# A two-layer trunk on one core: other rooms for the last output weights, and the last norms queued after the last tile

## The chip, the cores and the metric

The kernel runs on one core of one Trainium2 chip. The metric is device time in microseconds (us). A core has TensorE (PE, matmuls and transposes into PSUM, with the weight loads shown apart as PEld), VectorE (DVE), ScalarE (ACT) and GpSimd (POOL), and here SyncE (SP) issues nearly all the loads, with 16 DMA engines that move the bytes. Each engine takes its instructions in the order of its own queue and waits on semaphores for others.

## The reference

The trunk has two layers over 1024 positions of 1024 channels. Layer 0 mixes with an S5 scan and a GLU, layer 1 with a short gated convolution. Each is followed by the same FFN and a gated per-layer input (called ple below):

```python
for i in range(DEPTH):                      # DEPTH = 2
    hn = rmsnorm(h, norm_mix_g[i])
    mix = s5_mixer(hn, ...) if i % 2 == 0 else shortconv_mixer(hn, ...)
    h = h + mix
    h = h + swiglu_ffn(rmsnorm(h, norm_ffn_g[i]), ffn_w_in[i], ffn_w_out[i])
    gate = sigmoid(rmsnorm(h, norm_ple_g[i]) @ ple_w_gate[i])
    h = h + gate * (p[i] @ ple_w_up[i])
return rmsnorm(h, final_norm_g)
```

The hidden width of the FFN is 2816, and all of it is float32.

## The kernel before

**Precision and tiles.** Every matrix product is made from float32 operands split in two: `hi` is a cast (ACT, L87) and `lo` the remainder (a DVE subtraction, L88), and `mm3` (L122 to L124) adds three matmuls hi·hi, hi·lo and lo·hi. The 1024 positions are 8 tiles `t` of 128, taken in the order 0, 4, 1, 5, 2, 6, 3, 7. Tiles q and q+4 form pair q.

**Stages, by the trace.** S5 scan to about 225 us, GLU to 407, first FFN half (`ffn_in`) 420 to 848, second half (`ffn_out`) 848 to 1112, ple 1112 to 1206, then in layer 1 `conv_in` 1225 to 1470, `conv_out` 1480 to 1557, `ffn_in` 1571 to 1997, `ffn_out` 1998 to 2262, ple and the final norm to the end.

**The seven-product stages.** `ffn_in` and `conv_in` compute 2x2 blocks with seven products instead of eight (`block_product`). Their moving operands c = 0 to 6 are made from the normed tiles by `norm_pair` (L207): for each pair two scalings `xn` on DVE (L173), 16 transposes on PE (L181), four DVE subtractions (L221 to L232), and seven splits called `put(0)` to `put(6)`, each a cast on ACT and a subtraction on DVE (L88). c = 0 to 3 lie in `ulow`, c = 4 to 6 in `uhigh`. A product of one block is 12 matmuls. The weights come as two loads `raw` and are made into seven operands `ws` by casts, sums and splits (L275 to L283, L87, L88).

**The output stages.** `out_phase` (L326) serves `ffn_out` and `conv_out`. It keeps weight rows as split "units" in SBUF and runs through them in groups; for `ffn_out` these are units 0 to 7, 8 to 15 and 16 to 21, in `conv_out` 0 to 3 and 4 to 7. For each group it goes over the eight tiles: load the hidden activations (`ch`, one or two chunks of four units, L346), in group 0 also load the residual `h` (L348), multiply, and add into `h` on DVE (L360). In the last group the tile's sum of squares (L139) and `last_post` (L366) follow. The units of the next group are fetched (L330) while the group runs, one after each tile, if their room is free ("early"), otherwise after the group's last tile. The rooms are eight slots in `ulow` (units 0 to 7), six in `uhigh` (8 to 13), four in `s8` (14 to 17), and for units 18 to 21 again four of `uhigh`, which group 1 is still reading, so these four are late. The four gate units of ple take `uhigh` slots 4, 5, 0, 1, two early and two late.

**One ring for all loads.** Weights (`raw`), chunks (`ch`) and normed tiles (`xn`) share four slots r0 to r3 of a ring (`raw_tile`, L82), taken in turn in the order in which the program allocates them. A load's issue on SP waits for the last reader of its slot, and every DMA issue behind it on SP waits too.

**What orders the work.** The program's order and a list scheduler that works through a timeline give each engine its fixed queue; `first()` raises the priority of the sums and norms. `posted()` (L1010) makes `last_post`: where seven products follow, pair q's work is placed after tile q+1, and pair 3's after tile 7. Where ple follows, each tile's norm (`norm_tile`, into `s8` tiles) is placed after that tile.

Of the kernel before, what the change touches and what calls it, by code (L numbers as in the profile page):

```python
# [23 lines left out]
def trunk(  # L24
# [11 lines left out]
    T = S // P  # L36
# [95 lines left out]
    def square(t, cs):  # L132

        if "ms" not in squares:
            squares["ms"] = tiny.tile([P, T, 4], F32, name="ms", tag="ms")
        got = squares.setdefault(t, [])
        junk = t2_tile("junk", BF16, D)
        ms = squares["ms"][:, t, len(got):len(got) + 1]
        A.activation(junk[:, cs], h[t][:, cs], AF.Square, scale=1.0 / math.sqrt(D), accum_out=ms)  # L139
        got.append(ms)  # L140
# [66 lines left out]
    def norm_pair(q, gb):  # L207
        t0, t1 = q, q + HT
        halves = 2 if q == HT - 1 else 1
        x0, x1 = normed(t0, gb, halves), normed(t1, gb, halves)  # L210

        def put(c, src):
            split(moving_part(c, 0, q), moving_part(c, 1, q), by_kt(src))

        p11, p12, p22 = transposed(x0, 0), transposed(x1, 0), transposed(x1, 1)
        p21 = transposed(x0, 1, mm)
        put(0, p11)
        b12 = t2_tile("b12")
        A.copy(b12, p12)
        T1 = t2_tile("T1")  # L220
        V.tensor_tensor(T1, b12, p11, ALU.subtract)  # L221
        T2 = t2_tile("T2")
        V.tensor_tensor(T2, p22, T1, ALU.subtract)
        put(1, T2)
        put(2, T1)
        put(3, p21)
        T3 = t2_tile("T3")
        V.tensor_tensor(T3, p22, b12, ALU.subtract)
        put(4, T3)
        put(5, p22)  # L230
        T4 = t2_tile("T4")
        V.tensor_tensor(T4, p21, T2, ALU.subtract)  # L232
        put(6, T4)

# [54 lines left out]
    def block_product(ws, on_c11=None):  # L289


        def prod(ps, i, start):
            for kt in range(KH):
                sl = slice(kt * P, (kt + 1) * P)
                mm3(ps, ws[i][:, 0, sl], ws[i][:, 1, sl], moving(i, kt, 0), moving(i, kt, 1),
                    start and kt == 0, kt == KH - 1, more=not start)

        a = psum()
        prod(a, 0, True)
        s1 = ev_tile("s1")  # L300
# [25 lines left out]
    def out_phase(wout, groups, last_post, following=()):  # L326
# [4 lines left out]

        units = {ht: fetch(ht, room) for ht, room, _ in groups[0]}
        for gi, group in enumerate(groups):
# [5 lines left out]
            for t in ORDER:  # L339
# [7 lines left out]
                if gi == 0:  # L347
                    nc.sync.dma_start(out=h[t], in_=hdram[t])  # L348
                ps = [psum() for _ in range(2)]
                for j in parts:  # L350
                    mine = [x[0] for x in group if x[0] // 4 == j]
                    for nb in range(2):
# [5 lines left out]
                        if mine[-1] == group[-1][0]:  # L358
                            with first():
                                V.tensor_tensor(h[t][:, cs], ps[nb], h[t][:, cs], ALU.add)  # L360
                                if last:
                                    square(t, cs)
                if soon:
                    soon.pop(0)()
                if last:
                    last_post(t)  # L366
            for f in soon + late:
                f()

    def room_low(q, s):  # L370
# [25 lines left out]
    def ffn_out(l, post, following):  # L396
        rooms = [(room_low(q, s), False) for s in range(2) for q in range(HT)]
        rooms += [(room_high(i), True) for i in range(6)] + [(room_new(i), True) for i in range(4)]
        rooms += [(room_high(i), False) for i in range(4)]
        hts = [(ht, *room) for ht, room in enumerate(rooms)]  # L400
# [15 lines left out]
    def ple(l, units, post):  # L416
        more, makers = ple_units(l, 1, [room_new(i) for i in range(4)])
        for nb in range(2):
# [3 lines left out]
            for t in ORDER:  # L422
# [3 lines left out]
                for c0, c1 in ((0, 256), (256, 512)) if last else ((0, 512),):  # L426
# [4 lines left out]
                    with first():  # L431
                        A.activation(ps, ps, AF.Sigmoid)
                        V.tensor_tensor(upt[:, c0:c1], ps, upt[:, c0:c1], ALU.mult)
                        hc = slice(nb * 512 + c0, nb * 512 + c1)
                        V.tensor_tensor(h[t][:, hc], upt[:, c0:c1], h[t][:, hc], ALU.add)
                        square(t, hc)
# [44 lines left out]
    def glu(post):  # L481
# [3 lines left out]
        for nb in range(4):  # L485
# [8 lines left out]
            for t in ORDER:  # L494
# [5 lines left out]
                with first():  # L500
                    A.activation(sg, ps[:, 256:512], AF.Sigmoid)
                    V.tensor_tensor(sg, ps[:, 0:256], sg, ALU.mult)
                    V.tensor_tensor(h[t][:, cs], sg, h[t][:, cs], ALU.add)
                    square(t, cs)
# [505 lines left out]
    def posted(gain, pairs):  # L1010

        gb = load_gain(gain)

        def pair(q):
# [4 lines left out]
        def post(t):  # L1019
            if not pairs:  # L1020
                return norm_tile(t, gb)
            if 0 < t < HT:
                pair(t - 1)
            if t == T - 1:
                pair(HT - 1)
        return post
# [73 lines left out]
```

## Time and profile before

| | |
|---|---|
| Median of 3 runs | 2356.33 us (2354.39 to 2356.82) |
| Profiled execution | 2359.43 us, its span 2357.5 us |
| Mean granted TensorE clock | 0.981 |
| PE busy | 2247.0 us, 95% of the span |
| PEld, DVE, ACT, POOL busy | 78%, 56%, 32%, 7% |
| DMA moved | 288.87 MB, mean 123 GB/s |

PE's queue is busy for nearly the whole span, so time that is to be had lies in the stretches where PE stands still or where the clock granted to it is the lower of its two levels, 1.2 instead of 2.4 GHz (0.5 in the rows). A row of the timeline gives the start, the duration, the engine and line, the operation, and in brackets the idle time before it and what ended that. Matmuls overlap, so the pitch from start to start, and not the duration, is what one costs.

### The profile page before, as it was taken

The page shows a single profiled execution, that of the slowest core. Times are in us where ns is not written, and L with a number is a line of the kernel's source. Part 1 is how long each engine was busy: PE and PEld are TensorE (multiplying, and loading weights), DVE is VectorE, ACT ScalarE, POOL GpSimd, SP SyncE. Part 2 cuts the span into 40 slices and gives each one's busy share as a digit, 9 for nine tenths or more (in the row PEclk, how much of TensorE's full clock was granted, in tenths as well). Part 3 has the DMA queues.
Part 4 walks back from the last instruction along what each step waited for, and adds up shares of the span by engine and source line. Part 5 has one row for each costly group of instructions (what it writes and reads, how often), then busy time and mean ns, then how long its engine had stood idle before and what let it go on. Part 6 is the DMA issues. An engine that isn't in the chain of part 4 may idle for free.

```text
span 2357.5 us, 27090 instructions
## 1 busy us (share of the span) xinstructions
PE 2247.0 (95%) x10253; PEld 1835.7 (78%) x10253; DVE 1331.9 (56%) x2246; ACT 765.5 (32%) x1449; POOL 163.1 (7%) x268
## 2 busy tenths in 40 slices
PE   6888999899999999999979999989999999999998
PEld 4776887788888878878858888768888888788787
DVE  7785326866666642125488776487666666121454
ACT  6554223433333320013343332153333333000232
POOL 2110001000000000000000000010000001000000
PEclk8999999999999999999989999999999999999999
DMA  7555202333333364333232225434333335543333
GB/s 246 141 135 148 69 1 89 105 112 112 111 114 110 107 241 149 118 127 114 70 129 81 90 92 179 159 125 125 108 108 107 111 113 172 212 139 107 108 109 110
DMA packets 212978, 288.87 MB, mean 123 GB/s; under 512 B 21360, under 2 KB 152432, under 8 KB 212848
## 3 DMA queue, kind: packets, MB, share of 16 engines
q1 hardware_dynamic: 191520, 212.63, 29.0%
q0 software_dynamic: 20928, 74.47, 10.2%
q8 instruction: 80, 1.31, 0.2%
q14 instruction: 50, 0.41, 0.1%
q10 hardware_dynamic: 400, 0.04, 0.0%
HBM read 190.93 MB, written 79.69 MB: 115 GB/s over the span
## 4 chain that ended last, share of the span: by engine, by line
PE 85%; DMA 6%; DVE 5%; ACT 1%; SPq 1%; issue 1%; POOL 0%; DVEq 0%; POOLq 0%; ACTq 0%
PE psmm L122 27%; PE psmm L124 27%; PE psmm L123 27%; DMA ch<-hid 2%; PE pstr L181 1%; DMA raw<-in_ffn_w_out_dram 1%; DMA tw<-tmp 1%; DVE W L575 1%; DVE gv L925 1%; DMA h<-hd 1%; DVE tmp L575 1%; DVE ulow L88 1%; DVE uhigh L88 1%; PE pstr L874 0%; DVE raw L575 0%
## 5 line engine op out<-in xcount | busy, mean ns | idle before, releaser
L122 PE MATMUL psmm<-ulow,ws 128*128 128x512 f32 x896 | 351.1, 393 | 1.6 <-ACT s L301 1.6
L123 PE MATMUL psmm<-ulow,ws 128*128 128x512 f32 x896 | 350.6, 391 | 0.0
L124 PE MATMUL psmm<-ulow,ws 128*128 128x512 f32 x896 | 350.4, 391 | 0.0
L124 PE MATMUL psmm<-uhigh,ws 128*128 128x512 f32 x672 | 265.3, 395 | 0.0
L122 PE MATMUL psmm<-uhigh,ws 128*128 128x512 f32 x672 | 265.1, 394 | 0.0
L123 PE MATMUL psmm<-uhigh,ws 128*128 128x512 f32 x672 | 264.9, 394 | 0.0
L360 DVE TENSOR_TENSOR h<-psmm,h 128x512 f32<-128x512 f32 x128 | 88.0, 690 | 276.6 <-PE psmm L124 276.6
L88 DVE TENSOR_TENSOR ws<-raw,ws 128x512 fp32r<-128x512 f32 x224 | 153.6, 688 | 117.8 <-ACT ws L87 117.4
L87 ACT CAST ws<-raw 128x512 fp32r<-128x512 f32 x224 | 137.5, 619 | 213.0 <-PE psmm L124 211.2
L122 PEld LDWEIGHTS psmm<-ulow,ws 128*128 128x128 f32 x896 | 169.4, 189 | 39.5 <-ACT s L301 2.9
L123 PEld LDWEIGHTS psmm<-ulow,ws 128*128 128x128 f32 x896 | 169.4, 189 | 36.2
L124 PEld LDWEIGHTS psmm<-ulow,ws 128*128 128x128 f32 x896 | 169.2, 189 | 36.2
L87 ACT CAST ws<-st 128x512 fp32r<-128x512 f32 x168 | 104.0, 620 | 204.4 <-PE psmm L124 189.5
L123 PEld LDWEIGHTS psmm<-uhigh,ws 128*128 128x128 f32 x672 | 126.1, 188 | 30.3
L124 PEld LDWEIGHTS psmm<-uhigh,ws 128*128 128x128 f32 x672 | 126.1, 188 | 30.3
L122 PEld LDWEIGHTS psmm<-uhigh,ws 128*128 128x128 f32 x672 | 126.1, 188 | 29.1
L323 POOL DMA_DIRECT2D hid<-hs x104 | 78.2, 755 | 903.4 <-DVE hs L88 895.4
L122 PE MATMUL psmm<-ulow,ch 128*128 128x512 f32 x320 | 128.4, 401 | 10.8 <-DMA ch<-hid 10.8
L139 ACT ACTIVATE junk<-h 128x512 bf16<-128x512 f32 (+1 forms) x113 | 64.0, 567 | 204.0 <-DVE h L360 104.0
L87 ACT CAST uhigh<-raw 128x1024 fp32r<-128x1024 f32 x36 | 37.2, 1049 | 278.9 <-PE psmm L124 136.7
L123 PE MATMUL psmm<-ulow,ch 128*128 128x512 f32 x320 | 127.6, 399 | 0.0
L124 PE MATMUL psmm<-ulow,ch 128*128 128x512 f32 x320 | 127.5, 398 | 0.0
(240 smaller groups left out, 4238.5 us busy)
## 6 DMA issues: line engine op xcount, KB each, us to landing
hid<-hs POOLq DMA_DIRECT2D x104, 512.0 KB, 4.3
ch<-hid SPq DMA_DIRECT2D x96, 512.0 KB, 3.7
raw<-in_ffn_w_in_dram SPq DMA_DIRECT2D x88, 512.0 KB, 4.4
raw<-in_ffn_w_out_dram SPq DMA_DIRECT2D x44, 512.0 KB, 3.6
hd<-h POOLq DMA_DIRECT2D x24, 512.0 KB, 3.0
h<-hd SPq DMA_DIRECT2D x24, 512.0 KB, 8.7
raw<-in_conv_w_in_dram SPq DMA_DIRECT2D x24, 512.0 KB, 4.0
up<-ev SPq DMA_DIRECT2D x32, 256.0 KB, 3.2
```

What stands on the lines that cost most here:

```text
L87: A.copy(hi, src)
L88: V.tensor_tensor(lo, src, hi.bitcast(F32), ALU.subtract)
L122: PE.matmul(ps, ahi, bhi, start=start, stop=False, skip_group_check=more)
L123: PE.matmul(ps, ahi, blo, start=False, stop=False, skip_group_check=more)
L124: PE.matmul(ps, alo, bhi, start=False, stop=stop, skip_group_check=more)
L139: A.activation(junk[:, cs], h[t][:, cs], AF.Square, scale=1.0 / math.sqrt(D), accum_out=ms)
L181: PE.transpose(pt[:, c * P:(c + 1) * P], xn[:, kt * P:(kt + 1) * P], ident)
L323: nc.gpsimd.dma_start(out=hid[ht // 4][half * HT:(half + 1) * HT, :, ht % 4].rearrange("t p l j -> p t l j"), in_=hs.bitcast(F32))
L360: V.tensor_tensor(h[t][:, cs], ps[nb], h[t][:, cs], ALU.add)
L575: V.tensor_tensor(o, a, b, op)
L925: V.tensor_tensor_scan(gv[:, g, 1:P], dec, sv[:, g, 1:P], 0.0, ALU.mult, ALU.add)
```

## The change

Four things are edited. (1) Units 18 to 21 go to the `ulow` slots of units 2, 6, 3 and 7, which are free as soon as group 0 is done, and are early; the ple units go to `uhigh` slots 0 to 3 and are all early. (2) `out_phase` fetches six units of group 0, then issues the first tile's `ch` loads, then fetches units 6 and 7. `conv_out` has four units in its group 0 and is not touched by this. (3) In the last group, `last_post` of tiles 2, 6, 3 and 7 (t mod 4 of 2 and 3) is called after the loop over all the tiles, in `ffn_out` and `conv_out` both. (4) Where seven products follow, pair 2 and pair 3 are made together by `last_pairs`: the norms of tiles 2, 6 and 3 are queued at tile 3, and the rest with an ordering behind the last tile's sum and square; pair 3's second half of transposes is put behind the first product, and the stores of these four tiles come last.

```diff
     def ffn_out(l, post, following):
         rooms += [(room_high(i), True) for i in range(6)] + [(room_new(i), True) for i in range(4)]
-        rooms += [(room_high(i), False) for i in range(4)]
+        rooms += [(room_low(q, s), True) for q in (2, 3) for s in range(2)]
     def ffn_ple(l, last):
-        units, makers = ple_units(l, 0, [room_high(i) for i in (4, 5, 0, 1)])
-        ffn_out(l, posted(norm_ple_g[l], False), [(i < 2, f) for i, f in enumerate(makers)])
+        units, makers = ple_units(l, 0, [room_high(i) for i in range(4)])
+        ffn_out(l, posted(norm_ple_g[l], False), [(True, f) for f in makers])
     def out_phase(wout, groups, last_post, following=()):
-        units = {ht: fetch(ht, room) for ht, room, _ in groups[0]}
+        units = {ht: fetch(ht, room) for ht, room, _ in groups[0][:KT - 2]}
+        kept = []
...
                 if gi == 0:
                     nc.sync.dma_start(out=h[t], in_=hdram[t])
+                for ht, room, _ in groups[0]:
+                    if ht not in units:
+                        units[ht] = fetch(ht, room)
...
-                if last:
+                if last and t % HT < HT // 2:
                     last_post(t)
+                elif last:
+                    kept.append(t)
             for f in soon + late:
                 f()
+        for t in kept:
+            last_post(t)
     def last_pairs(xs, gb):
+        a, z = HT - 2, HT - 1
+        with tc.issue_after(done["sum"]), tc.issue_after(done["square"]):
+            xs[T - 1] = normed(T - 1, gb, 2)
+            p = {(0, 0): transposed(xs[a], 0), (1, 0): transposed(xs[a + HT], 0), (1, 1): transposed(xs[a + HT], 1),
+                 (0, 1): transposed(xs[a], 1, mm)}
+            put(0, a, p[0, 0])
+            r = {(0, i): transposed(xs[z], i, mm) for i in range(2)}
+            put(0, z, r[0, 0])
+            others(a, p)
+            n = len(tc.nc.cur_bb.bb.instructions)
+            r.update({(1, i): transposed(xs[T - 1], i) for i in range(2)})
+            held[:] = [i for i in tc.nc.cur_bb.bb.instructions[n:] if i.engine == PE.engine]
+            others(z, r)
     def post(t):
-            if 0 < t < HT:
+            if 0 < t < HT - 1:
                 pair(t - 1)
+            if t == HT - 1:
+                xs.update({i: normed(i, gb) for i in (HT - 2, T - 2, HT - 1)})
             if t == T - 1:
-                pair(HT - 1)
+                last_pairs(xs, gb)
+                for i in (HT - 2, T - 2, HT - 1, T - 1):
+                    spill(i)
```

How the queues move is shown at three places. The first is SP's queue at the start of `ffn_out` in layer 0 (`raw` are weights, `ch` chunks of hidden blocks `hid0` and `hid1`, `h` residual tiles). Before:

```order
L100 DMA raw_6815<-in_ffn_w_out_dram 128x1024
L346 DMA ch_6819<-hid0_99 128x1024
L346 DMA ch_6821<-hid1_100 128x1024
L100 DMA raw_6876<-in_ffn_w_out_dram 128x1024
L348 DMA h_6777<-hd_98 128x1024
L348 DMA h_6778<-hd_98 128x1024
L346 DMA ch_6880<-hid0_99 128x1024
L348 DMA h_6779<-hd_98 128x1024
...
L348 DMA h_6784<-hd_98 128x1024
L346 DMA ch_6882<-hid1_100 128x1024
L346 DMA ch_6941<-hid0_99 128x1024
```

After:

```order
L372 DMA ch_6810<-hid0_99 128x1024
L372 DMA ch_6812<-hid1_100 128x1024
L100 DMA raw_6815<-in_ffn_w_out_dram 128x1024
L100 DMA raw_6819<-in_ffn_w_out_dram 128x1024
L372 DMA ch_6881<-hid1_100 128x1024
L374 DMA h_6776<-hd_98 128x1024
...
L100 DMA raw_6936<-in_ffn_w_out_dram 128x1024
...
L100 DMA raw_6875<-in_ffn_w_out_dram 128x1024
...
L374 DMA h_6783<-hd_98 128x1024
L372 DMA ch_6879<-hid0_99 128x1024
```

The second tile's chunks were ch_6880 (its first half) and ch_6882 (its second); now they are ch_6879 (first half) and ch_6881 (second). The first half has moved from ahead of six `h` loads to behind all eight and two weight loads, and its ring slot is the one that the first tile's second chunk, ch_6812, sits in.

The second place is SP's queue at the end of group 1 (`hid2` and `hid3` belong to group 1, `hid4` and `hid5` to group 2). Before:

```order
L346 DMA ch_7711<-hid2_101 128x1024
L346 DMA ch_7713<-hid3_102 128x1024
L100 DMA raw_7767<-in_ffn_w_out_dram 128x1024
L100 DMA raw_7771<-in_ffn_w_out_dram 128x1024
L100 DMA raw_7775<-in_ffn_w_out_dram 128x1024
L346 DMA ch_7783<-hid4_103 128x1024
L346 DMA ch_7785<-hid5_104 128x512
```

After:

```order
L100 DMA raw_7666<-in_ffn_w_out_dram 128x1024
L372 DMA ch_7728<-hid3_102 128x1024
L372 DMA ch_7672<-hid3_102 128x1024
L372 DMA ch_7726<-hid2_101 128x1024
L372 DMA ch_7782<-hid4_103 128x1024
L372 DMA ch_7784<-hid5_104 128x512
```

The weight loads that stood between the last chunks of group 1 and the first of group 2 are gone from there; they now stand one by one between the tiles of group 1.

The third place is DVE's queue at the end of `conv_out` (the sums into `h` are L360 before and L389 after, `put` steps L88, and `h_10833` after, like `h_10835` before, is the last tile). Before:

```order
L360 TENSOR_TENSOR h_10835<-psmm_11537,h_10835 128x512
L173 SCALAR_TENSOR_TENSOR xn_11573<-h_10834,rs_11571,gb_10836 128x512 x2
L360 TENSOR_TENSOR h_10835<-psmm_11538,h_10835 128x512
L221 TENSOR_TENSOR T1_11513<-b12_11511,pstr_11489 128x512
L223 TENSOR_TENSOR T2_11515<-pstr_11499,T1_11513 128x512
L228 TENSOR_TENSOR T3_11523<-pstr_11499,b12_11511 128x512
```

After:

```order
L389 TENSOR_TENSOR h_10833<-psmm_11420,h_10833 128x512
L144 TENSOR_SCALAR ms_11137<-ms_11137 128x1
L173 SCALAR_TENSOR_TENSOR xn_11519<-h_10831,rs_11517,gb_10834 128x1024
L88 TENSOR_TENSOR ulow_81<-pstr_11463,ulow_81 128x4x128
L146 TENSOR_TENSOR ms_11137<-ms_11137 128x1
L173 SCALAR_TENSOR_TENSOR xn_11525<-h_10832,rs_11523,gb_10834 128x1024
L221 TENSOR_TENSOR T1_11487<-b12_11485,pstr_11463 128x512
L88 TENSOR_TENSOR ulow_81<-psmm_11478,ulow_81 128x4x128
```

Behind the last tile's sums there used to stand the four subtractions and seven splits of pair 2 and the work of pair 3. Now pair 1's four subtractions and seven splits (its first is the `ulow` split from pstr_11463) and two more scalings `xn` stand there as well.

## Rows read from the trace of the kernel before

**Rows 1.** The page, busy time of the engines over the whole span.
```profile
PE 2247.0 (95%) x10253; PEld 1835.7 (78%) x10253; DVE 1331.9 (56%) x2246; ACT 765.5 (32%) x1449; POOL 163.1 (7%) x268
```

**Rows 2.** PE's waits: waiting line, releaser, total us, times, longest us.
```profile
PE pstr L181 <- DVE xn L173: 36.0, 5, 10.7
PE psmm L122 <- DMA ch<-hid: 19.9, 7, 4.6
```

**Rows 3.** PE's timeline at the end of group 1, layer 0, then layer 1.
```profile
1040.22 0.50 PE L123 MATMUL psmm<-uhigh,ch 128*128 128x512 f32 x1 [0.53 <-DVE uhigh L88]
...
1045.66 0.80 PE L122 MATMUL psmm<-w,ch 128*128 128x512 f32 x1 [4.24 <-DMA ch<-hid]
...
2188.66 0.50 PE L123 MATMUL psmm<-uhigh,ch 128*128 128x512 f32 x1 [0.45 <-DVE uhigh L88]
...
2194.22 0.79 PE L122 MATMUL psmm<-w,ch 128*128 128x512 f32 x1 [4.35 <-DMA ch<-hid]
```

**Rows 4.** SP's timeline at the end of group 1 (durations are issue times).
```profile
1033.29 0.42 SPq L100 DMA_DIRECT2D raw<-in_ffn_w_out_dram  x1
1039.01 1.50 SPq L346 DMA_DIRECT2D ch<-hid  x3
```

**Rows 5.** Stretches: length, busy of PE, PEld, DVE, ACT, POOL, clock, DMA, GB/s.
```profile
848.00:859.00 11.00, 11.00 (x48) 8.95 (x48) 6.05 (x8) 2.31 (x4) 1.50 (x2) 1.00 0.97 345
859.00:870.00 11.00, 6.41 (x27) 4.94 (x26) 0.69 (x1) 0.00 (x0) 0.56 (x1) 0.88 1.03 417
...
1046.00:1052.00 6.00, 6.00 (x15) 4.63 (x15) 1.23 (x1) 1.05 (x1) 0.00 (x0) 0.52 0.14 40
...
2008.00:2019.00 11.00, 7.55 (x31) 5.82 (x30) 0.69 (x1) 0.00 (x0) 0.56 (x1) 0.94 1.02 414
...
2194.00:2200.00 6.00, 5.78 (x16) 4.59 (x17) 1.23 (x1) 1.05 (x1) 0.00 (x0) 0.61 0.21 67
```

**Rows 6.** PE's timeline, first matmul of the second tile of group 0, both layers.
```profile
869.58 0.80 PE L122 MATMUL psmm<-ulow,ch 128*128 128x512 f32 x1 [4.59 <-DMA ch<-hid]
...
2018.07 0.80 PE L122 MATMUL psmm<-ulow,ch 128*128 128x512 f32 x1 [3.45 <-DMA ch<-hid]
```

**Rows 7.** SP's timeline at the start of `ffn_out`, layer 0.
```profile
848.97 0.32 SPq L346 DMA_DIRECT2D ch<-hid  x1
849.34 3.57 SPq L348 DMA_DIRECT2D h<-hd  x6
853.94 1.59 SPq L346 DMA_DIRECT2D ch<-hid  x2
```

**Rows 8.** DVE's timeline, the second sum of the first tile, both layers.
```profile
859.45 0.69 DVE L360 TENSOR_TENSOR h<-psmm,h 128x512 f32<-128x512 f32 x1 [2.10 <-PE psmm L124]
...
2009.05 0.69 DVE L360 TENSOR_TENSOR h<-psmm,h 128x512 f32<-128x512 f32 x1 [2.11 <-PE psmm L124]
```

**Rows 9.** Tile `ch` from 838 to 885 us, issue to landing of its loads.
```profile
DMA to landing us min/median/max: 3.3/5.3/15.6
```

**Rows 10.** PE's timeline, last transposes before the seven products, GLU then `conv_out`.
```profile
418.95 1.97 PE L181 MATMUL pstr<-ident,xn 128*128 128x128 f32 x8 [10.42 <-DVE xn L173]
...
1569.69 1.97 PE L181 MATMUL pstr<-ident,xn 128*128 128x128 f32 x8 [10.71 <-DVE xn L173]
```

**Rows 11.** Stretches from last to first product: GLU, ple, `conv_out`; columns of rows 5.
```profile
406.50:420.60 14.10, 3.68 (x26) 3.29 (x24) 12.44 (x22) 7.67 (x16) 1.13 (x2) 0.75 0.42 136
1206.40:1225.60 19.20, 4.41 (x25) 3.62 (x25) 16.10 (x27) 7.66 (x16) 2.35 (x6) 0.65 0.44 144
1557.00:1571.30 14.30, 3.58 (x25) 3.24 (x24) 11.31 (x20) 6.49 (x14) 1.44 (x2) 0.74 0.48 147
```

**Rows 12.** DVE's timeline at the end of `conv_out`: a scaling, then steps in a row.
```profile
1552.69 1.27 DVE L173 SCALAR_TENSOR_TENSOR xn<-h,rs,gb 128x1024 f32<-128x1024 f32 x1
...
1560.89 0.68 DVE L88 TENSOR_TENSOR ulow<-pstr,ulow 128x512 fp32r<-128x512 f32 x1
1561.49 0.68 DVE L232 TENSOR_TENSOR T<-psmm,T 128x512 f32<-128x512 f32 x1
1562.09 1.28 DVE L88 TENSOR_TENSOR ulow<-T,ulow 128x512 fp32r<-128x512 f32 x2
```

More of the change, by code (lines that the diff above doesn't have):

```diff
@@ L138, in square @@
         ms = squares["ms"][:, t, len(got):len(got) + 1]
-        A.activation(junk[:, cs], h[t][:, cs], AF.Square, scale=1.0 / math.sqrt(D), accum_out=ms)
+        done["square"] = A.activation(junk[:, cs], h[t][:, cs], AF.Square, scale=1.0 / math.sqrt(D), accum_out=ms).ins
         got.append(ms)
@@ L207, in norm_pair @@
     def norm_pair(q, gb):
[L208 to L217, printed above, removed]
+        x0, x1 = normed(q, gb), normed(q + HT, gb)
+        p = {(0, 0): transposed(x0, 0), (1, 0): transposed(x1, 0), (1, 1): transposed(x1, 1), (0, 1): transposed(x0, 1, mm)}
@@ L218, in norm_pair, with put, others @@
+        put(0, q, p[0, 0])
+        others(q, p)
+    def put(c, q, src):
+        split(moving_part(c, 0, q), moving_part(c, 1, q), by_kt(src))
+    def others(q, p):
         b12 = t2_tile("b12")
-        A.copy(b12, p12)
+        A.copy(b12, p[1, 0])
         T1 = t2_tile("T1")
-        V.tensor_tensor(T1, b12, p11, ALU.subtract)
+        V.tensor_tensor(T1, b12, p[0, 0], ALU.subtract)
         T2 = t2_tile("T2")
-        V.tensor_tensor(T2, p22, T1, ALU.subtract)
-        put(1, T2)
-        put(2, T1)
@@ L226, in norm_pair @@
-        put(3, p21)
+        V.tensor_tensor(T2, p[1, 1], T1, ALU.subtract)
+        put(1, q, T2)
+        put(2, q, T1)
+        put(3, q, p[0, 1])
         T3 = t2_tile("T3")
-        V.tensor_tensor(T3, p22, b12, ALU.subtract)
-        put(4, T3)
-        put(5, p22)
+        V.tensor_tensor(T3, p[1, 1], b12, ALU.subtract)
+        put(4, q, T3)
+        put(5, q, p[1, 1])
         T4 = t2_tile("T4")
-        V.tensor_tensor(T4, p21, T2, ALU.subtract)
-        put(6, T4)
+        V.tensor_tensor(T4, p[0, 1], T2, ALU.subtract)
@@ new lines, in others, with last_pairs @@
+        put(6, q, T4)
+    done = {}
+    held = []
+    def last_pairs(xs, gb):
+        a, z = HT - 2, HT - 1
[11 more added lines that the diff above has]
+            others(z, r)
@@ L299, in block_product @@
         prod(a, 0, True)
+        product = next(i for i in reversed(tc.nc.cur_bb.bb.instructions) if i.engine == PE.engine)
+        while held:
+            tc.add_manual_dep(held.pop(), product.name,
+                              mybir.DependencyInfo(mybir.DependencyClass.NoSync, mybir.DependencyReason.DATA),
+                              reason="behind the first product")
         s1 = ev_tile("s1")
@@ L359, in out_phase @@
                             with first():
-                                V.tensor_tensor(h[t][:, cs], ps[nb], h[t][:, cs], ALU.add)
+                                done["sum"] = V.tensor_tensor(h[t][:, cs], ps[nb], h[t][:, cs], ALU.add).ins
                                 if last:
@@ L434, in ple @@
                         hc = slice(nb * 512 + c0, nb * 512 + c1)
-                        V.tensor_tensor(h[t][:, hc], upt[:, c0:c1], h[t][:, hc], ALU.add)
+                        done["sum"] = V.tensor_tensor(h[t][:, hc], upt[:, c0:c1], h[t][:, hc], ALU.add).ins
                         square(t, hc)
@@ L502, in glu @@
                     V.tensor_tensor(sg, ps[:, 0:256], sg, ALU.mult)
-                    V.tensor_tensor(h[t][:, cs], sg, h[t][:, cs], ALU.add)
+                    done["sum"] = V.tensor_tensor(h[t][:, cs], sg, h[t][:, cs], ALU.add).ins
                     square(t, cs)
@@ L1012, in posted @@
         gb = load_gain(gain)
+        xs = {}
         def pair(q):
```

## The prediction

> **What bounds the kernel now.** I read the page first: PE is busy for 95% of the span [rows 1], so time can only come from PE's gaps and from stretches at the lower clock. The list of PE's waits names the gaps that this change can touch: 36.0 us in five waits of transposes for a normed tile, and 19.9 us in seven waits of matmuls for a chunk `ch` [rows 2]. The timelines place them. Two of the `ch` waits stand where group 1 of `ffn_out` passes to group 2, 4.24 and 4.35 us long [rows 3], two where group 0 goes from its first tile to its second, 4.59 and 3.45 us [rows 6]; the waits for `xn` stand before the seven-product stages [rows 10]. The change works on all three kinds, so each is costed apart.
>
> **Group 1 to group 2, twice: a gain.** Before, PE stops first 0.53 and 0.45 us for the split of a late unit, then 4.24 and 4.35 us for the first chunk of group 2 [rows 3]. The reason stands on SP: a weight load goes out at 1033.29, the next chunks only at 1039.01 to 1040.5 [rows 4], because their ring slots hold late weights that DVE must split first, and a load takes 3.3 us at least [rows 9]. After the stall PE runs at the lower clock. In the stretch from 1046 the granted clock is 0.52 and 15 matmuls take 6.00 us; in the one from 2194 it is 0.61 and 16 take 5.78 [rows 5]. At the higher clock 48 take 11.00, so 0.229 each [rows 5], and 15 or 16 would take 3.44 or 3.66. The lower clock costs 2.6 and 2.1. With the change the late loads are gone, and the first chunks of group 2 wait only for PE to leave a slot about a tile and a half ahead. The six fetches that now stand between group 1's tiles are of the kind that already stands between group 0's, where I find no PE gap beyond the second tile. What goes is 0.53 + 4.24 + 2.6 = 7.4 in layer 0 and 0.45 + 4.35 + 2.1 = 6.9 in layer 1: **-14.3** in sum. If the clock dips for another cause, the 4.7 of clock stay, so the bounds are -9.5 and -15.
>
> **Start of `ffn_out`, twice: a loss.** Before, SP issues a chunk of the second tile at 848.97 and the other at 853.94, after six more `h` loads [rows 7]; this second one takes the longest of all, 15.6 us [rows 9], and PE waits 4.59 us for it, halfway through the tile. DMA is full meanwhile: shares of 0.97 and 1.03, 345 and 417 GB/s from 848 to 870 [rows 5]. With six units ahead of the chunks instead of eight, the ring turns by two. The second tile's first chunk now lands in the slot that the first tile's second chunk occupies until that tile is finished. That is at 859.45, when DVE can add it [rows 8], and in layer 1 at 2009.05. So it cannot be issued until PE has run out of work, and PE waits for the whole of its transfer. By rows 9 that is 3.3 us at best and 15.6 at worst, a change of the wait from 4.59 of between -1.3 and +11.0. I take the landing from the bytes: up to it DMA must move the same eight `h` loads and nearly the same weights and chunks as up to 869.58 before, one 512 KB load more or less, which at 417 GB/s is 1.3 us. SP also stands a few us behind two weight loads whose slots come free late. So it lands near 870, the wait is 870 - 859.45 = 10.5, and the loss is 10.5 - 4.6 = 5.9. In layer 1 the chunk landed at 2018.07 and DMA was as full (1.02, 414 GB/s [rows 5]); a landing at 2019 makes the wait 10.0 instead of 3.45, a loss of 6.6. In sum **+12.5**, bounds -1.5 and +23, in practice +6 to +18. What hides nothing here is the earlier arrival of the second half.
>
> Rows 9 show loads of one size at 3.3 and at 15.6 us; rows 7 and 5 show which one stood behind many. The Trainium skill, page "DMA: Bandwidth & Descriptors", section "Queues, rings and completion order", says that each DMA engine consumes descriptors in ring order, which agrees with the 15.6. The same page's section "Anatomy of one DMA" prices a load at about 2 us plus its bytes over 436 GB/s, an estimate of 3.2 us for 512 KB with nothing ahead. The sum stands without these sentences.
>
> **Before the seven products: three places.** The last pair's operands are bound by DVE. In the stretch from the last matmul to the first product DVE is busy 12.44 of 14.10 us after the GLU, 16.10 of 19.20 after ple, 11.31 of 14.30 after `conv_out` [rows 11]. The new order can only fill the rest, since pair 2's and pair 3's steps are as many as before.
>
> After the GLU that rest is 1.7 us. Pair 2's steps no longer stand ahead of the last tile's sum, the first product can begin before pair 3's second half is transposed, but its weights are split by the same DVE: I take **-1.6**, bounds -4 and +1. After ple the rest is 3.1, but two weight loads of `conv_in` now stand on SP ahead of the last tile's `upt` load, and DVE's first weight sum ahead of that tile's sum; the weight loads wait for the transposes of `xn` tiles that share the ring. I take **-1.0**, bounds -3 and +2.
>
> After `conv_out` it is otherwise. There `out_phase` itself holds back the posts of tiles 2, 6, 3 and 7, and the post of tile 2 is the one that makes pair 1. So pair 1's eleven DVE steps come behind the last sums, with two more scalings. A step is 0.60 from start to start and a scaling 1.27 [rows 12]: 11 x 0.60 + 2 x 1.27 = 9.1 us. They can fill the 14.30 - 11.31 = 3.0 us in which DVE waited. **+6.1** remains. The upper bound is 9.1. The lower one is about +1: the first product's operands need only `put(0)` of each pair, and 12 matmuls at the lower clock, some 5 us, may cover part of it. I keep 6.1, because the next products need pair 1's and pair 2's other operands, and those stand behind everything else on DVE. The 16 transposes of pair 1 leave the matmul stretch and come back behind it, so they count for nothing.
>
> **`ffn_out` to ple, twice: nothing.** The norms of tiles 2, 6, 3 and 7 now follow the last sum, but ple begins with tiles 0, 4, 1 and 5, whose 4 x 24 matmuls at 0.229 [rows 5] are 22 us of cover; four scalings at 1.27 and 16 splitting steps at 0.60 [rows 12] are 15 us. If the cover fails, about 2 us are lost. The ple weights, now all early, leave the end of group 2. Zero, bounds -1 and +2.
>
> **Sum.** -14.3 + 12.5 - 1.6 - 1.0 + 6.1 + 0 = **+1.7 us**. The profiled execution took 2359.43, 3.1 above the median of 2356.33; the sum is a difference and is set against the median: 2358.0.
>
> **Rivals.**
> *The second tile's chunk lands at once.* If DMA has drained by the time PE frees the slot, the load takes 3.3 us [rows 9] and the waits are shorter than before: -1.3 and -0.2 in place of +12.5, so 1.7 - 14.0 = -12.3, 2344. For it: SP is held up at several points, so DMA has less queued. Against it: the same bytes kept DMA at 1.03 to 870 [rows 5]. Chance 0.22. The lone-load price in the Trainium skill, page "DMA: Bandwidth & Descriptors", section "Anatomy of one DMA", would make the same case, with waits of 3.2 us.
> *The chunk lands late.* Between the `h` loads SP now waits for the split of unit 7 and for PE to leave the first chunk. If those waits come late enough to leave DMA idle for 3 us, the chunk lands near 874, each wait is some 14 us, and the loss is 9 to 11 each instead of 6. The sum is 1.7 + 8 = +10, 2366. It decides from a landing of about 872. Chance 0.20.
> *Pair 1's work is covered after all.* PE takes the first products while DVE catches up; the 6.1 shrinks to 1, and the GLU gives 3. Sum -5, 2351. For it: PE has nothing else to wait for at that point. Against it: DVE is busy 79% of that stretch already [rows 11]. Chance 0.10.
> *The change doesn't do what it says.* Units 18 to 21 come early but the first chunks of group 2 still wait, for a slot that DVE or SP holds. The 14.3 stay, and the sum is +16, 2372. The order shows no weight load between the last chunks of group 1 and the first of group 2, which speaks against it. Chance 0.05.
>
> **How the numbers follow.** The forecast has 0.43; its own range, from the inner bounds of its terms, is about -4 to +8 us, 2352 to 2364. A measurement of this kernel tells about 0.2%, 4.7 us, from no change, so "same" is 2351.6 to 2361.0. Of the forecast's 0.43, 0.33 falls there, 0.09 above and 0.01 below. The first rival is faster (0.22), the second slower (0.20), the third half faster and half same (0.05 each), the fourth slower (0.05). Faster 0.28, same 0.38, slower 0.34. The range for 8 times in 10 leaves out the fourth rival and the outer parts of the first two: 2344 to 2368.
>
> **What would show it.** In the profile after: no PE wait over 1 us and no drop of the clock near the end of group 1; one wait of about 10 us for `ch` after the first tile of `ffn_out`, at both layers, with DMA full until it ends; about 6 us more from the last matmul of `conv_out` to where PE is again continuous, with DVE nearly without gaps; the gap after the GLU shorter by 1 to 2. The forecast is wrong if the wait after the first tile is under 6 or over 13 us, or if pair 1's work turns out to lie ahead of the last sums.

## The result and the profile after

The changed kernel takes 2367.81 us (median of 4 runs, 2366.73 to 2371.47), the kernel before 2356.57 on the same chip: a ratio of 1.0047, with a 95% interval from 1.0032 to 1.0063. It is slower by about 11 us. That lies at the upper end of the range on record, and is not the "no change" that was the forecast.

The list of PE's waits in the profile after (waiting line, releaser, total us, times, longest) answers to [rows 2]:

```profile
PE psmm L122 <- DMA ch<-hid: 28.3, 3, 13.6
PE psmm L122 <- ACT ws L87: 22.0, 4, 8.2
...
PE psmm L124 <- DVE ws L88: 5.7, 2, 4.4
PE psmm L122 <- ACT ulow L87: 5.5, 2, 4.4
...
PE psmm L181 <- DVE xn L173: 4.3, 2, 3.3
...
PE pstr L181 <- DVE xn L173: 0.3, 1, 0.3
```

The 36.0 us of transposes that wait for `xn` have become waits of the products themselves, for weights and operands (`ws`, `ulow`). The waits for `ch` are fewer, three instead of seven, and longer, 28.3 us instead of 19.9.

To see where time went, one compares the same matmuls in both traces. The matmuls L122 to L124 come in the same number, 8952, in all the kernels, so the time from the start of the n-th to that of the m-th is a stretch that can be set side by side. The table gives such stretches around the places of the prediction, in us, for the profiled executions (the kernels e1 to e11 are told of below).

| kernel | to the GLU's end | GLU to `ffn_in` | start of `ffn_out`, layer 0 | group 1 to 2, layer 0 | ple to `conv_in` | `conv_out` to `ffn_in` | start of `ffn_out`, layer 1 | group 1 to 2, layer 1 |
|---|---|---|---|---|---|---|---|---|
| before | 398.8 | 35.5 | 35.0 | 55.8 | 101.9 | 60.4 | 33.1 | 55.9 |
| after | 394.5 | 34.8 | 42.4 | 48.1 | 106.1 | 65.8 | 43.4 | 48.1 |
| difference | -4.4 | -0.7 | +7.4 | -7.8 | +4.2 | +5.4 | +10.3 | -7.8 |
| forecast | 0 | -1.6 | +5.9 | -7.4 | -1.0 | +6.1 | +6.6 | -6.9 |
| e1 | 394.2 | 33.9 | 33.4 | 48.0 | 105.7 | 68.0 | 34.6 | 48.1 |
| e2 | 393.4 | 35.6 | 44.2 | 54.4 | 101.8 | 60.9 | 43.0 | 54.1 |
| e3 | 396.6 | 35.6 | 34.7 | 48.0 | 102.1 | 61.1 | 33.3 | 48.1 |
| e4 | 396.3 | 34.2 | 44.6 | 48.0 | 105.1 | 69.8 | 44.6 | 48.1 |
| e5 | 395.0 | 34.9 | 35.0 | 54.7 | 106.5 | 68.0 | 35.1 | 56.2 |
| e6 | 394.3 | 35.6 | 35.0 | 48.0 | 101.9 | 65.9 | 33.2 | 48.1 |
| e7 | 394.3 | 35.4 | 28.1 | 48.0 | 102.1 | 60.9 | 28.0 | 48.1 |
| e8 | 394.3 | 34.1 | 35.1 | 48.0 | 105.7 | 65.8 | 35.8 | 48.1 |
| e9 | 396.5 | 34.1 | 34.9 | 54.4 | 103.4 | 67.8 | 35.2 | 56.5 |
| e10 | 396.7 | 35.6 | 28.0 | 56.1 | 102.1 | 61.7 | 28.0 | 54.9 |
| e11 | 394.5 | 34.6 | 28.0 | 48.0 | 102.0 | 61.5 | 28.0 | 48.1 |

The first column isn't the change's: the profiled execution of before was 2.9 us above its median, and all the other kernels, with any part of the change or none of it in that stretch, come to the GLU's end 2 to 5 us sooner than that one execution. Without it the differences add to 11.0, and 0.5 us more lies in the stretches that the table leaves out (+0.8 in the two that hold the passage from `ffn_out` to ple, -0.3 in the others). That makes 11.5, close to the 11.2 us between the medians.

**The gain is there.** In the profile after, stretches around the end of group 1 in both layers (columns as in [rows 5]) show PE without a gap, at the full clock:

```profile
1030.00:1050.00 20.00, 20.00 (x88) 16.12 (x87) 6.74 (x10) 3.55 (x6) 0.56 (x1) 1.00 0.33 119
2180.00:2200.00 20.00, 20.00 (x88) 16.29 (x88) 3.90 (x5) 1.05 (x1) 0.00 (x0) 1.00 0.33 110
```

Before, the same places had a clock of 0.52 and 0.61 [rows 5] and the four gaps of [rows 3].

**The waits at the start of `ffn_out` are there too, and longer than forecast.** PE's timeline after, the second tile's first matmul in both layers, to be set beside [rows 6]:

```profile
866.94 0.80 PE L122 MATMUL psmm<-ulow,ch 128*128 128x512 f32 x1 [12.85 <-DMA ch<-hid]
...
2026.87 0.80 PE L122 MATMUL psmm<-ulow,ch 128*128 128x512 f32 x1 [13.63 <-DMA ch<-hid]
```

SP's timeline after shows the order that leads there; [rows 7] are its counterpart:

```profile
844.00 0.33 SPq L372 DMA_DIRECT2D ch<-hid  x1
844.38 1.37 SPq L374 DMA_DIRECT2D h<-hd  x3
845.86 0.37 SPq L100 DMA_DIRECT2D raw<-in_ffn_w_out_dram  x1
846.33 1.13 SPq L374 DMA_DIRECT2D h<-hd  x2
848.53 0.33 SPq L100 DMA_DIRECT2D raw<-in_ffn_w_out_dram  x1
848.91 2.31 SPq L374 DMA_DIRECT2D h<-hd  x3
854.12 2.97 SPq L372 DMA_DIRECT2D ch<-hid  x2
```

The chunk that PE needs goes out at 854.12, when the first tile is done, behind eight `h` loads and two weight loads. It lands 12.8 us later. The issue before that of 844.00 was at 839.24; in between SP stood for the other chunk, whose slot unit 6 held until DVE had split it, and all that is queued behind it stood too. What DMA did meanwhile is seen in stretches that hold the same matmuls. The change's trace runs 5.2 us ahead of that of before in layer 0, and 4.2 behind it in layer 1, so the first two rows of the second fence, layer 0 and 1, belong beside 848 to 859 in [rows 5] (a DMA share of 0.97) and beside this row of before:

```profile
1998.00:2009.00 11.00, 11.00 (x49) 8.86 (x48) 4.45 (x6) 2.19 (x3) 1.51 (x2) 1.00 1.00 381
```

```profile
842.80:853.80 11.00, 11.00 (x49) 8.83 (x47) 5.67 (x7) 2.19 (x3) 1.50 (x2) 1.00 0.77 266
2002.20:2013.20 11.00, 11.00 (x48) 8.63 (x46) 5.73 (x7) 3.09 (x4) 1.50 (x2) 1.00 0.74 267
...
859.00:867.00 8.00, 0.06 (x1) 0.06 (x1) 1.23 (x1) 1.04 (x1) 0.00 (x0) 0.50 1.03 414
```

After the change DMA stands at a share of 0.77 and 0.74 where it was 0.97 and 1.00, and is full afterwards, when PE has nothing to do and its clock is the lower one (0.50).

**After ple there is a loss that I had forecast as a gain.** DVE's timeline at the end of ple comes first, before the change (L433 multiplies the last tile's up chunk, L435 is its sum) and after it (L466 and L468, with the first weight step of `conv_in`, L295). SP's issue of that up chunk follows, and then PE's timeline after:

```profile
1217.73 0.69 DVE L88 TENSOR_TENSOR uhigh<-pstr,uhigh 128x512 fp32r<-128x512 f32 x1
1218.33 0.68 DVE L433 TENSOR_TENSOR upt<-psmm,upt 128x512 f32<-128x512 f32 x1
...
1220.72 0.68 DVE L435 TENSOR_TENSOR h<-upt,h 128x512 f32<-128x512 f32 x1
```

```profile
1209.61 0.69 DVE L295 TENSOR_TENSOR st<-raw 128x512 f32<-128x512 f32 x1 [3.85 <-DMA raw<-in_conv_w_in_dram]
1210.22 0.69 DVE L466 TENSOR_TENSOR upt<-psmm,upt 128x512 f32<-128x512 f32 x1
...
1211.43 0.69 DVE L468 TENSOR_TENSOR h<-upt,h 128x512 f32<-128x512 f32 x1
```

```profile
1203.05 0.53 SPq L457 DMA_DIRECT2D upt<-up  x1
```

```profile
1215.87 0.79 PE L122 MATMUL psmm<-ulow,ws 128*128 128x512 f32 x1 [8.08 <-ACT ws L87]
...
1218.43 0.79 PE L124 MATMUL psmm<-ulow,ws 128*128 128x512 f32 x1 [1.35 <-DVE ws L88]
...
1230.49 1.65 PE L122 MATMUL psmm<-ulow,ws 128*128 128x512 f32 x3 [4.42 <-ACT ulow L87]
```

DVE stands 3.85 us for a weight load, and behind it stand the last sum and all of pair 2's and pair 3's steps. The up chunk came hardly sooner: issued at 1203.05, it took 7.15 us and landed at 1210.20, just before L466. PE then starts the products early, 16.0 us after ple's last matmul instead of 19.2, and stops in them for 1.35 and 4.42 us.

### The profile page after: what moved, and what is told of

It is laid out like the page before. It is cut to its first block, busy times and chain, and to the rows that moved or that the text cites. A ratio compares the mean times of both kernels' runs of the same rounds, so it can differ in the third digit from the quotient of the medians.

```text
span 2364.7 us, 27087 instructions
## 1 busy us (share of the span) xinstructions
PE 2246.1 (95%) x10253; PEld 1836.2 (78%) x10253; DVE 1332.1 (56%) x2243; ACT 766.7 (32%) x1449; POOL 162.4 (7%) x268
## 4 chain that ended last, share of the span: by engine, by line
PE 89%; DVE 5%; DMA 4%; ACT 1%; issue 1%; SPq 0%; DVEq 0%; POOL 0%; POOLq 0%; ACTq 0%
PE psmm L122 28%; PE psmm L123 28%; PE psmm L124 28%; DMA ch<-hid 1%; PE pstr L181 1%; DVE W L608 1%; PE pstr L973 1%; PE pstr L974 0%; DVE gv L958 0%; PE pstr L975 0%; DVE ulow L88 0%; DMA W<-W 0%; PE pstr L907 0%; DMA tw<-tmp 0%; DVE tmp L608 0%
## 5 line engine op out<-in xcount | busy, mean ns | idle before, releaser
L122 PE MATMUL psmm<-ulow,ws 128*128 128x512 f32 x896 | 353.7, 396 | 27.5 <-ACT ws L87 22.0
L124 PE MATMUL psmm<-ulow,ws 128*128 128x512 f32 x896 | 352.8, 394 | 5.7 <-DVE ws L88 5.7
L124 PE MATMUL psmm<-uhigh,ws 128*128 128x512 f32 x672 | 265.4, 395 | 0.0
L122 PE MATMUL psmm<-uhigh,ws 128*128 128x512 f32 x672 | 264.9, 394 | 0.0
L389 DVE TENSOR_TENSOR h<-psmm,h 128x512 f32<-128x512 f32 x128 | 88.3, 691 | 271.9 <-PE psmm L124 271.9
L122 PEld LDWEIGHTS psmm<-ulow,ws 128*128 128x128 f32 x896 | 170.7, 191 | 66.4 <-ACT ws L87 23.1
L88 DVE TENSOR_TENSOR ws<-raw,ws 128x512 fp32r<-128x512 f32 x224 | 153.3, 687 | 113.8 <-ACT ws L87 113.8
L122 PE MATMUL psmm<-ulow,ch 128*128 128x512 f32 x448 | 178.2, 399 | 29.1 <-DMA ch<-hid 28.3
L124 PEld LDWEIGHTS psmm<-ulow,ws 128*128 128x128 f32 x896 | 170.3, 190 | 43.8 <-DVE ws L88 7.5
L123 PE MATMUL psmm<-ulow,ch 128*128 128x512 f32 x448 | 178.2, 398 | 0.0
L124 PE MATMUL psmm<-ulow,ch 128*128 128x512 f32 x448 | 177.7, 397 | 0.0
L124 PEld LDWEIGHTS psmm<-uhigh,ws 128*128 128x128 f32 x672 | 126.1, 188 | 30.2
L122 PEld LDWEIGHTS psmm<-uhigh,ws 128*128 128x128 f32 x672 | 126.1, 188 | 29.1
L122 PEld LDWEIGHTS psmm<-ulow,ch 128*128 128x128 f32 x448 | 85.1, 190 | 50.6 <-DMA ch<-hid 27.4
```

Of the source, the lines that this page charges most:

```text
L88: V.tensor_tensor(lo, src, hi.bitcast(F32), ALU.subtract)
L122: PE.matmul(ps, ahi, bhi, start=start, stop=False, skip_group_check=more)
L123: PE.matmul(ps, ahi, blo, start=False, stop=False, skip_group_check=more)
L124: PE.matmul(ps, alo, bhi, start=False, stop=stop, skip_group_check=more)
L389: done["sum"] = V.tensor_tensor(h[t][:, cs], ps[nb], h[t][:, cs], ALU.add).ins
```

## The experiments

**e1: the change without its second part.** Fetch all of group 0 first, as before.

```diff
-        units = {ht: fetch(ht, room) for ht, room, _ in groups[0][:KT - 2]}
+        units = {ht: fetch(ht, room) for ht, room, _ in groups[0]}
```

> The changed kernel with its second part alone undone: all eight units of group 0 are fetched before the first tile's chunks, as before. Theory: the waits of 12.8 and 13.6 us for the second tile's first chunk come from the ring slot that the first tile's second chunk holds. Comparing the two traces, the two starts of ffn_out cost 7.5 and 10.3 us, so this kernel should gain 17.8 on the changed one, 2367.8 - 17.8 = 2350, and show chunk waits of about 4.6 and 3.5 us there as before the change. Rival: the waits come from the deferred posts or from DMA being busy otherwise, and the order of fetches is worth only the 12.5 us that was forecast or less: 2355 or more.

Measured: 2352.78 us, ratio to before 0.9984 (0.9975 to 0.9994), so 15 us come back. The starts of `ffn_out` are again at 33.4 and 34.6 us. The theory holds for these two places; they give back 17.8. The 3 us that are missing by time lie mostly at the end of `conv_out`, 68.0 against 65.8 with all parts.

**e2: the second part alone**, on the kernel before, by the same edit the other way round.

> The kernel before with the second part alone: six units, the first tile's chunks, then the last two units. Theory: the same two waits appear without any other part, 2356.6 + 17.8 = 2374.4, with one wait of 12 to 14 us for a chunk after the first tile of ffn_out in each layer. Rival: the size needs the other parts too (the rooms or the deferred posts), and it costs the forecast 12.5 or less: 2369 or less.

Measured: 2375.22 us, ratio 1.0072 (1.0057 to 1.0087), 19 us more than before on that chip. PE's timeline shows the two waits without any other part of the change:

```profile
868.60 0.79 PE L122 MATMUL psmm<-ulow,ch 128*128 128x512 f32 x1 [14.71 <-DMA ch<-hid]
...
2025.62 0.79 PE L122 MATMUL psmm<-ulow,ch 128*128 128x512 f32 x1 [13.44 <-DMA ch<-hid]
```

Order of fetches alone makes them; the rival that the rooms or the deferred posts are needed is out.

**e3: the rooms alone**, with the deferred posts that they need in `ffn_out` and nowhere else.

```diff
-        rooms += [(room_high(i), False) for i in range(4)]
+        rooms += [(room_low(q, s), True) for q in (2, 3) for s in range(2)]
-                if last:
+                if last and (len(groups) == 2 or t % HT < HT // 2):
                     last_post(t)
+                elif last:
+                    kept.append(t)
```

> The kernel before with the first part alone: units 18 to 21 in the low rooms, loaded early, the gate units of ple early, and for that the posts of tiles 2, 6, 3 and 7 after the loop in ffn_out only; fetch order, conv_out and the pairs as before. Theory: both stalls at the end of group 1 go with the stretch at the lower clock behind them, 7.6 and 7.8 us by the two traces, and nothing comes in their place: 2356.6 - 15.4 = 2341. Rival: the deferred posts of ffn_out cost 2 to 5 us at the start of ple: 2343 to 2346.

Measured: 2342.60 us, ratio 0.9935 (0.9919 to 0.9952), 13.4 us less than before. That lies between the theory (2341) and the rival (2343 to 2346), and the traces decide: both stretches of group 1 to 2 are 7.8 us shorter, and the two stretches behind them, which the table leaves out and which hold the passage to ple, are 0.5 and 0.3 us longer. So the deferred posts in `ffn_out` are covered but for 0.8, not the rival's 2 to 5.

**e4: the whole change, but `conv_out` calls its posts at once.**

```diff
-                if last and t % HT < HT // 2:
+                if last and (len(groups) == 2 or t % HT < HT // 2):
```

> The changed kernel, but conv_out calls the post of each tile at once, so that pair 1's work lies among its last matmuls again; ffn_out still defers. Theory: pair 1's eleven steps and two scalings behind the last sum cost 5.3 us by the two traces: 2367.8 - 5.3 = 2362.5. Rival: that loss is made by the hold-back of the last two pairs, which stays: 2366 to 2368.

Measured: 2374.15 us, ratio 1.0069 (1.0054 to 1.0084): 6 us slower than the change, where the theory had 5 faster. It fell. PE's timeline of this kernel shows a new wait among the last matmuls of `conv_out`:

```profile
1554.90 0.80 PE L122 MATMUL psmm<-w,ch 128*128 128x512 f32 x1 [2.93 <-DMA ch<-hid]
...
1572.14 0.79 PE L122 MATMUL psmm<-ulow,ws 128*128 128x512 f32 x1 [6.38 <-ACT ws L87]
```

The held-back pairs take three slots of the ring for the `xn` of tiles 2, 6 and 3 at tile 3, where pair 2 alone took two. So the last tile's chunk comes into the slot of tile 3's chunk, which PE reads up to its matmul at 1551.14; it was issued at 1551.57 and landed at 1554.86. With the posts deferred, the `xn` tiles are made after the last chunk and this wait is not there. By the table 4.0 of the 6 us lie at `conv_out`. The starts of `ffn_out` are 2.2 and 1.2 us longer as well, which this edit doesn't touch; why is not known.

**e5: the fourth part alone**, the held-back pairs at all three places, with everything else as before.

> The kernel before with the fourth part alone: the last two pairs made together and held behind the last tile's sum and square, at the ends of the GLU, of ple and of conv_out; rooms, fetch order and posts as before. Theory: this part itself is what costs at two of the three places, 4.1 us after ple (a load of weights and the late sum on DVE's queue) and, by the run with conv_out's posts at once, 9.5 us after conv_out, against a gain of 0.7 after the GLU: 2356.3 + 13 = 2369. Rival: the fourth part alone is worth the 1.6 and 1.0 that I forecast and what costs is only its meeting with the deferred posts: 2354.

Measured: 2365.87 us, ratio 1.0041 (1.0026 to 1.0056), 9.9 us slower. By the table the GLU gains 0.6, ple loses 4.6, `conv_out` 7.7 and the start of layer 1's `ffn_out` 2. So the part that makes the last norms start sooner is itself a loss at two of its three places. At `conv_out` it has the wait of e4, by PE's timeline:

```profile
1553.31 0.80 PE L122 MATMUL psmm<-w,ch 128*128 128x512 f32 x1 [2.97 <-DMA ch<-hid]
```

**e6: the rooms and the deferred posts in `conv_out`, pairs as before.** This is e3 with

```diff
-                if last and (len(groups) == 2 or t % HT < HT // 2):
+                if last and t % HT < HT // 2:
```

> The rooms alone (2342.6) plus the deferred posts in conv_out, with the pairs made as before, so that pair 1, pair 2 and pair 3 all follow the last matmul one by one. This is the step that I priced at 6.1. Theory by my sum: 9.1 us of DVE work behind the last sum less what fills gaps, 2342.6 + 6 to 9 = 2349 to 2352. Rival: the first products cover it and it costs 0 to 2: 2343 to 2345.

Measured: 2348.86 us, ratio 0.9973 (0.9959 to 0.9987), 6.3 us above e3, with runs from 2346.1 to 2354.8, and the stretch at `conv_out` is 65.9 against 61.1, 4.8 more. That is near the term as I had priced it, 6.1, and here it stands alone.

**e7: the rooms, and the `h` loads spread.** The load of a tile's `h` in group 0 is queued on SP behind that tile's chunks (`issue_after` orders a queue and adds no wait).

```diff
-                        nc.sync.dma_start(out=ch[:, ks].bitcast(F32), in_=hid[ht // 4][t, :, ks])
+                        chunk = nc.sync.dma_start(out=ch[:, ks].bitcast(F32), in_=hid[ht // 4][t, :, ks]).ins
                 if gi == 0:
-                    nc.sync.dma_start(out=h[t], in_=hdram[t])
+                    with tc.issue_after(chunk):
+                        nc.sync.dma_start(out=h[t], in_=hdram[t])
```

> The rooms alone (2342.6) with one more edit: in group 0 the load of a tile's residual h is queued on SP behind that tile's own chunks, so the eight loads no longer go out together ahead of the second tile's second chunk. Theory: the two waits of 4.6 and 3.5 us that this chunk has before the change come from the loads queued ahead of it, and go with the stretch at the lower clock behind them, some 2 us each: 2342.6 - 8 to 12 = 2331 to 2335. Rival: DMA is full there with weights and stores anyway and the waits stay: 2341 to 2343.

Measured: 2327.17 us, ratio 0.9876 (0.9861 to 0.9890), 15.4 us below e3 and 28.8 below before. In the stretches of [rows 5] PE is now never idle and its clock stays up, with DMA less full than there:

```profile
848.00:859.00 11.00, 11.00 (x49) 8.85 (x48) 2.65 (x4) 0.19 (x1) 1.79 (x3) 1.00 0.91 321
859.00:870.00 11.00, 11.00 (x49) 8.86 (x48) 2.61 (x3) 1.56 (x2) 0.00 (x0) 1.00 0.62 212
```

No wait for `ch` is left in PE's list. The gain is larger than 8 to 12, since `conv_out` begins in the same way and gains some 2 us as well, and since the two starts of `ffn_out` give 6.6 and 5.3.

**e8: the whole change with the `h` loads spread**, by the same edit.

> The whole changed kernel with that same edit of the h loads. The ring slot still keeps the second tile's first chunk from going out before the first tile is done, but fewer loads stand ahead of it. Theory: of the waits of 12.8 and 13.6 us the slot itself makes only the time of one load, 3.3 to 5 us, and the rest is queueing behind the h loads: 2367.8 - 16 to 19 = 2349 to 2352, with two waits of 3.3 to 5. Rival: the slot and SP's own waits make most of it, and the waits stay at 8 or more: 2359 or more.

Measured: 2349.86 us, ratio 0.9974 (0.9964 to 0.9985), 18 us less than the change. The list of waits has

```profile
PE psmm L122 <- DMA ch<-hid: 10.9, 2, 5.5
```

This splits the wait: 5.5 and 5.4 us (layer 0 and 1) are the ring slot, which lets the load go out only when PE has run out of work, with the time of the load itself, which still has two `h` loads and two weight loads ahead of it; the other 7.4 and 8.2 went with the six `h` loads that were moved behind.

**e9: the fourth part with one repair after ple.** `conv_in`'s first two weight loads are queued on SP behind the last tile's up chunk, their vector steps behind the last sum.

```diff
-                ws = weights_set(tile_of(1, ct), tile_of(2, ct))
+                if ct == 0:
+                    with tc.issue_after(done["up"]), tc.issue_after(done["sum"]):
+                        ws = weights_set(tile_of(1, ct), tile_of(2, ct))
```

> The fourth part alone (2365.9) with one repair after ple: the first two weight loads of conv_in are queued on SP behind the last tile's up chunk, and their vector steps behind the last tile's sum. In the changed kernel's trace the sum waited for that chunk, which landed 7.15 us after its issue behind two weight loads, and DVE stood 3.85 us. Theory: the chunk lands in about 2.7 us, the last sum comes 3 to 4 us earlier, and most of the 4.1 us lost there comes back: 2362 to 2363, and the first matmuls of conv_in are again at the distance from ple's last that they have before. Rival: the weights then come later by as much, the first product waits for them, and nothing comes back: 2365 to 2366.

Measured: 2365.43 us, ratio 1.0043 (1.0029 to 1.0057), which by time can't be told from e5 and lies where the rival put it. The trace tells more: the stretch from ple to `conv_in` falls from 106.5 to 103.4 us, so 3.2 of the 4.6 come back. The last sum now stands here on DVE, with no gap of 3.85 ahead of it:

```profile
1204.46 1.28 DVE L173 SCALAR_TENSOR_TENSOR xn<-h,rs,gb 128x1024 f32<-128x1024 f32 x1 [0.75 <-POOL rs L148]
1205.66 0.68 DVE L466 TENSOR_TENSOR upt<-psmm,upt 128x512 f32<-128x512 f32 x1
1206.38 0.69 DVE L468 TENSOR_TENSOR h<-upt,h 128x512 f32<-128x512 f32 x1
```

The loads of the up chunks there, from issue to landing (least, median, most), first in the change, then in e9:

```profile
DMA to landing us min/median/max: 2.7/4.9/7.2
```

```profile
DMA to landing us min/median/max: 2.6/2.6/2.7
```

So by the trace two things of the fourth part made most of the loss after ple, the chunk behind two weight loads on SP and the weight step ahead of the sum on DVE, and this run undoes them together. Each alone would have held the last sum nearly as long: in the change the weights let DVE go on at 1209.61, and the chunk landed at 1210.20.

**e10: the spread `h` loads alone**, on the kernel before.

> The kernel before with nothing but the h loads queued behind each tile's own chunks. Theory: what they cost at the start of each ffn_out and of conv_out has nothing to do with the rooms: 2356.0 - 15.4 = 2340.6, as much as on top of the rooms. Rival: a part of the gain needs the early units, and it is 10 or less: 2346 or more.

Measured: 2342.07 us, ratio 0.9946 (0.9932 to 0.9959), 12.4 us less than before. That lies between the theory (15.4) and the rival (10), and the interval holds both. In the table the starts of `ffn_out` are 7.0 and 5.1 us shorter than before, as much as in e7 against e3 (6.6 and 5.3), so at these two places the gain doesn't need the rooms. The waits for `ch` that are left are the two at the end of group 1:

```profile
PE psmm L122 <- DMA ch<-hid: 8.7, 2, 4.7
```

**e11: rooms, spread `h` loads, and the held-back pairs after the GLU alone.**

> Rooms and spread h loads (2327.2), and the pairs held back at the end of the GLU alone, where the two traces show a gain of 0.7 us. Theory: 2326.5, not to be told from 2327.2 by time, with 0.5 to 1 us less from the GLU's last matmul to a continuous PE. Rival: the hold-back loses there too, 2 us or more: 2329 or more.

Measured: 2326.12 us, ratio 0.9880 (0.9866 to 0.9893), the same as e7 by time. The stretch after the GLU is 34.6 against 35.4, so 0.8 us of gain are to be seen in the trace.

## Why the prediction was right and wrong

The range held the time, with 0.2 us to spare, and the runs lie on both sides of its end (2366.7 to 2371.5); the terms missed by +9.8 us together, so that it held was in part luck. The forecast of no change was wrong: slower had 0.34. One of the signs of being wrong that I had set down, a wait of over 13 us after the first tile, came in layer 1 (13.63) and nearly in layer 0 (12.85). By its steps:

**Group 1 to group 2: right.** The forecast was -14.3, the table has -15.6, and e3, which has nothing else but the deferred posts of `ffn_out`, 13.4 by time. The clock came back with the gaps.

**Start of `ffn_out`: the mechanism right, the size too small.** The sum had +12.5, the table has +17.7, e2 by itself 19. The step that failed is the landing of the chunk. I took it from the bytes, with DMA as full as before up to that moment. DMA was not: around the time that SP waited for unit 6 its share was 0.77 instead of 0.97, and 0.74 instead of 1.00 in layer 1. Over 11 us that is 2.2 and 2.9 us of DMA work that came later, and the waits are 2.3 and 3.6 us longer than the 10.5 and 10.0 of the sum. I wrote that SP stands behind weight loads whose slots come free late, and gave it no price. The rival in which the chunk lands late had put 14 us of wait for that; 12.85 and 13.63 were measured, nearly that case. e8 shows that 5.5 of the wait was the slot with the load itself, and that the rest went with the order of the queue.

**After the GLU: right in sign.** -1.6 was forecast, -0.7 in the change and -0.8 in e11 was seen.

**After ple: wrong.** -1.0 was forecast and +4.2 measured, a miss of 5.2 at one place, as large as that of both starts of `ffn_out`. The step was that the new order can only fill the gaps of DVE, since pair 2's and pair 3's steps are as many as before. The steps are as many, but the gaps are not fixed: before, DVE did pair 2's work while the last tile's up chunk and the first weights were on their way, and with the work held behind the last sum it stood 3.85 us instead. I saw the two weight loads ahead of that chunk in SP's queue, and, with the order on DVE and the ring, priced them at 2 us. e9 puts the chunk and the sum first and takes back 3.2 of the 4.6 us that the fourth part costs there.

**After `conv_out`: the size near, the reason only half.** +6.1 was forecast, +5.4 measured. The stretch of the table can be cut at the last matmul of `conv_out`. Before, 26.1 us lie ahead of that matmul and 34.3 behind it; in the change 23.5 and 42.3, in e6 23.6 and 42.4, in e5 30.4 and 37.7. So the deferred posts alone (e6) make all that the change has here: 8.1 us more behind, and 2.6 less ahead, where transposes of pair 1 no longer stand among the matmuls. I had 9.1 us of steps less 3.0 of gaps behind, and nothing for the transposes; the two errors nearly cancel. In the 30 us after the last matmul DVE has gaps before, and is all but full in the change and in e6, in this order:

```profile
1556.70:1586.70 30.00, 19.06 (x86) 15.53 (x86) 25.32 (x44) 16.36 (x32) 1.44 (x2) 0.83 0.41 123
```

```profile
1553.00:1583.00 30.00, 16.66 (x75) 12.63 (x74) 29.71 (x50) 16.84 (x32) 2.03 (x2) 0.78 0.28 88
```

```profile
1542.70:1572.70 30.00, 18.50 (x74) 13.43 (x73) 29.39 (x49) 17.07 (x32) 1.50 (x2) 0.72 0.29 88
```

The held-back pairs alone cost 7.7 in this stretch (e5), which I had at nothing: 4.3 ahead of the last matmul, where the last chunk comes late as in e4, and 3.4 behind it. With the posts deferred that wait is gone, and DVE is full already: against e6 (65.9) the pairs add nothing in the change and in e8 (65.8 both), so the two don't add. In e1, which has both as well, they add 2.1 (68.0). Its PE comes back from its last long stop as soon as the change's, 23.8 and 24.1 us after the last matmul, but in the 12 us behind that its granted clock is 0.59 against 0.73; why it stays low for longer there was not tried.

**`ffn_out` to ple: right.** The deferred norms lie under ple's first tiles; e3 has them and loses 0.8 us at the two places, within the bounds.

The sum of the terms was +1.7. The misses are +5.2 after ple, +5.2 at the starts of `ffn_out`, +0.9 after the GLU, -0.7 after `conv_out`, -1.3 at the groups, and 0.5 in the rest: together +9.8, which makes 11.5 as in the table, against 11.2 by the medians.

## What to carry to other kernels

A change that lets loads start earlier also turns the ring that they share: follow who sits in the slot that the next load needs, and count what stands ahead of it in the queue. Work that is held behind a last step leaves its engine idle until that step's own inputs have come, so price the arrival of those first. And where many loads of one kind go out together ahead of one that is needed sooner, queue each behind the load that its tile needs first: here that was worth 12.4 us alone, nearly as much as the rooms (13.4).

## What the runs showed that I had not expected

No engine's list of waits names the `h` loads, yet spreading them gave 15.4 us on top of the rooms. A chunk took 3.3 to 7.2 us from issue to landing at the start of `ffn_out` with the loads spread, and up to 15.6 without [rows 9]; of the 12.85 us wait in the change, the loads ahead made 7.4. The Trainium skill's page "DMA: Bandwidth & Descriptors", section "Anatomy of one DMA", prices a DMA that GpSimd issues at about 2 us plus its bytes over 436 GB/s, which makes an estimate of 3.2 us for 512 KB. These loads are issued on SP, and their least of 3.3 agrees all the same; with more loads ahead the same chunk took 5.4 (e8) and 12.8 us (the change). And undoing a costly part within the change (e4) made it 6 us slower, 4.0 of it at `conv_out`, where that part had kept the `xn` tiles out of the last chunk's way.
